# Sample tokens of an SSD scan in four row strips: one product for both parts of y, and state products as row tiles

## The chip, the cores and the metric

The kernel runs on one core of one Trainium2 chip. The metric is the device time of one execution in microseconds (us). A core has five engines that work side by side: PE (TensorE, the matrix products; its weight loads are listed apart as PEld), DVE (VectorE), ACT (ScalarE), POOL (GpSimd) and SP (SyncE, which here only issues DMAs). Before, three executions took 1623.5, 1624.79 and 1626.45 us, median 1624.79 us.

## The reference, cut to what matters

One inference step of a two-layer decoder: a Mamba-2 SSD layer, then a pooling layer, each with its own projections, gates and norms. It takes one prompt sequence of 1024 tokens and eight sample sequences of 8 new tokens each, so 64 sample tokens. The change touches the SSD scan of the sample tokens. For each of 32 heads (8 groups of 4, head dimension 64, state dimension 128), with `h` the state of one sequence:

```python
# h_t = exp(dt_t A) h_{t-1} + dt_t x_t B_t^T,   y_t = h_t C_t
y_intra = einsum('bctsgr,bcsgrp->bctgrp', CB[..., None] * decay, xdt)     # within the 8 tokens
chunk_states = einsum('bctgn,bctgr,bctgrp->bcgrpn', B, decay_end, xdt)    # what they add to the state
y_inter = einsum('bctgn,bctgr,bcgrpn->bctgrp', C, exp(acum), h_prev)      # what the old state gives
y = y_intra + y_inter;   h_final = chunk_decay * h_prev + chunk_states
```

The outputs include y of all tokens, and the new state of the prompt and of each of the eight sample sequences.

## The kernel before, in words

All activations lie with features on the 128 partitions and the 1088 tokens (1024 prompt, then 64 sample) along the row. The large projections run as three products of float32r halves (hi x hi, hi x lo, lo x hi; L182 to L184 and L980 to L982), one pass each; plain float32 products take two passes, and transposes one.

`ssd_layer` walks the eight groups g. For each, `scan_group` is a generator that is cut into steps by its yields, and between two steps the kernel puts one or more units of other work for PE: projections of later groups, and from group 4 on parts of the output projection (`FILL` says how many after each step; one projection unit is 24 products of 352 or 368 columns). So PE's queue alternates between short scan work and long runs of L182 to L184. The program text gives each instruction a place; the build's scheduler keeps dependent work in order and may put an instruction earlier in its engine's queue when its inputs are ready. Each engine then executes its queue strictly in order.

In a group, chunks 0 to 7 are 128 prompt tokens each, chunk 8 is the 64 sample tokens.

- `front(c)` (L534 to L576) makes for a chunk C·B (L545), the transposes of the two x tiles and of B (L549), the decay matrix M (L556 to L560) and the scaled x, `xd`, in two versions: times dt, and times dt and the decay to the chunk's end (L562). It takes a PSUM bank with the tag `tr` (two buffers).
- In chunk 8 the transposes are made twice, by `dup` (L434 to L437): the 64 tokens appear in partitions 0 to 63 and again in 64 to 127. The second copy is used for a product in two halves, hi and lo, in one pass over 128 rows.
- `states(c)` (L583) makes the prompt's chunk states S (L588) and the running state h: hd on POOL (L596), h on DVE (L597). `rows(c)` makes y of two chunks (L609, L613) with column tiles of 64.
- `sample_inter` (L617 to L633), after the rows of chunks 6 and 7: 8 products of 32-column tiles give Z, the old state times C, for four pairs of sequences in four strips of 32 partitions, of which 16 are used (L628); DVE scales it to `zsc` (L631).
- `back_sample` (L635 to L654) makes y of the sample tokens: in each of two PSUM banks (tag `y`, two buffers) two products of `xdt` and M over 64 rows (L641), then two of `zsc` and a selection matrix over 128 rows (L644); DVE adds the bank to x (L580). Then POOL multiplies the old states by their decay (L647, two instructions of 128x1024), ACT and DVE make `st`, hi in partitions 0 to 63 and lo in 64 to 127 (L652, L653).
- `state_sample(half)` (L656 to L667) runs twice, one step apart: for each of two pairs of sequences ACT makes two masked copies of `st` (L660), PE multiplies them by B in hi and lo (L663, 2 products of 128x512), DVE adds the bank (tags `S` and `y`) to the old state (L665); a DMA sends the half out (L666).
- After the first of them come the gate and its squares (L700 to L702), after the second the mean square (L708), the norm and its round trip through memory (L713, L716), and the next group has begun by then.

At the head of the kernel, `dt_phase` (L439 to L501) computes dt, its running sum and the decay, and transposes them for prompt chunks (L493) and, by `dup`, for the sample tokens (L496).

Of the kernel before, what the change touches and what calls it, by code (L numbers as in the profile page):

```python
# [7 lines left out]
F32 = mybir.dt.float32  # L8
F32R = mybir.dt.float32r
# [50 lines left out]
K_ID, K_MASK, K_SMASK, K_SEL9, K_SEL64, K_SCAN, K_SEQ, K_CNT = 0, 128, 256, 320, 330, 394, 714, 722  # L60
K_N = 782
# [36 lines left out]
class Build:  # L98
# [335 lines left out]
    def dup(self, out, ap):  # L434

        for h in (0, 64):
            self.nc.tensor.matmul(out[h:h + 64], ap, self.ident, start=True, stop=True, tile_position=(0, h))  # L437

    def dt_phase(self, ps):  # L439
# [48 lines left out]
        self.tk.update({("x", cc): self.gp.tile([P, 2, (128, 128, 32)[cc]], F32, tag=f"tkx{cc}", name=f"tkx{cc}") for cc in range(3)})  # L488
        for i, src in enumerate((ac, dt, de)):
# [6 lines left out]
            self.dup(ps[:, :128], src[:, 256:320])  # L496
            nc.vector.tensor_copy(ds[2], ps[:, 96:128])
# [6 lines left out]
    def scan_group(self, g, T):  # L504
# [29 lines left out]
        def front(c):  # L534
# [8 lines left out]
            nc.scalar.activation(ea[:, :, :L], acb, AF.Exp)  # L543
            pt = pp.tile([P, 512], F32, tag="tr", bufs=2, name=self.name("tr"))
            nc.tensor.matmul(pt[:L, 384:384 + L], B[:, tok], C[:, tok], start=True, stop=True)  # L545
            for i, t in enumerate((xs[0], xs[1], B)):
                o = pt[:, 128 * i:128 * i + 128]
                if c < 8:
                    nc.tensor.transpose(o, t[:, tok], self.ident)  # L549
                else:  # L550
                    self.dup(o, t[:, tok])

            M = gp.tile([P, 4, 128], F32, tag="M", bufs=3, name=self.name("M"))
            mask = self.kc[:L, K_MASK:K_MASK + 128] if c < 8 else self.kc[:64, K_SMASK:K_SMASK + 64]
            for r in range(4):
                nc.scalar.activation(M[:L, r, :L], acb[:L, r, :], AF.Relu, bias=tk["ac", cc][:L, col + r:col + r + 1], scale=-1.0)  # L556
            nc.scalar.activation(M[:L, :, :L], M[:L, :, :L], AF.Exp, scale=-1.0)
            cb = gp.tile([P, 128], F32, tag="cb", bufs=1, name=self.name("cb"))
            nc.vector.tensor_tensor(out=cb[:L, :L], in0=pt[:L, 384:384 + L], in1=mask, op=ALU.mult)
            nc.vector.tensor_tensor(out=M[:L, :, :L], in0=M[:L, :, :L], in1=cb[:L, :L].unsqueeze(1).to_broadcast([L, 4, L]), op=ALU.mult)  # L560
# [74 lines left out]
        def back_sample(F, zsc):  # L635
            tok, M, xdt, xde, Bt, _, ea = F
            for q in range(2):
# [1169 lines left out]
```

## Time and profile before

| | us |
|---|---|
| median of three executions (1623.5 to 1626.45) | 1624.79 |
| the profiled execution | 1625.1 |
| its span, first to last instruction | 1623.2 |
| PE busy | 1594.8 |
| DVE busy | 1290.4 |
| ACT busy | 815.2 |
| POOL busy | 497.8 |

The span is one execution on the chip as the hardware profiler saw it. A row of the timeline reads: start in us from the span's beginning, length in us, engine, line of the kernel, operation, output <- inputs by their names, shapes, how many instructions were merged into the row, and in brackets how long the engine was idle before it and what released it. For PEld, `128*64` means that the weights have 128 rows and 64 columns, and the merged row ends with the last load's end. A row of the groups (by line) ends in busy us and the mean ns of one instruction. A row of the windows view has the stretch, its length, and for PE, PEld, DVE, ACT and POOL the busy us with the number of instructions, then the granted clock of PE, the share of DMA time and GB/s.

### The profile page before, as it was taken

To read this page: it belongs to the slowest core of one execution; us is meant where nothing else is said; L and a number is where in the kernel's file an instruction comes from. 1 tells how busy PE (TensorE), PEld (TensorE's weight loads), DVE (VectorE), ACT (ScalarE), POOL (GpSimd) and SP (SyncE) were. 2 spreads that over 40 slices of the span, in tenths; PEclk is the share of its full clock that TensorE was granted. 3 is DMA by queue.
4 is the path that set the end of the run, shared out by engine and by line. 5 is a ranking of instruction groups with operands and counts; after the bars stand their busy time and mean duration, and the time that the engine had idled before them with its cause. 6 is when DMAs were issued, how large, how long until landed. Compare 5 with 4: busy or idle time off the path is not lost.

```text
span 1623.2 us, 30975 instructions
## 1 busy us (share of the span) xinstructions
PE 1594.8 (98%) x12061; PEld 1519.9 (94%) x12061; DVE 1290.4 (79%) x2140; ACT 815.2 (50%) x1565; POOL 497.8 (31%) x527
## 2 busy tenths in 40 slices
PE   8999999999999999999999999999999999999997
PEld 6899999998889898898899899999999999999997
DVE  6875779777787888889878867988899867577886
ACT  6653444357667667675555536632322233333364
POOL 0233556421221302120112222366667640000241
PEclk9999999999999999999999999999999999999999
DMA  9422232354554554678899633043333369665773
GB/s 348 163 99 82 94 110 71 107 198 128 194 161 159 166 190 134 215 226 295 272 333 313 216 130 112 29 143 111 103 108 100 134 206 362 181 159 182 160 175 121
DMA packets 122306, 275.60 MB, mean 170 GB/s; under 512 B 18192, under 2 KB 59312, under 8 KB 122160
## 3 DMA queue, kind: packets, MB, share of 16 engines
q1 hardware_dynamic: 118128, 260.91, 47.4%
q0 software_dynamic: 4032, 12.72, 4.5%
q8 instruction: 95, 1.56, 0.4%
q14 instruction: 51, 0.42, 0.1%
HBM read 201.12 MB, written 70.23 MB: 167 GB/s over the span
## 4 chain that ended last, share of the span: by engine, by line
PE 83%; DVE 6%; DMA 4%; issue 3%; ACT 3%; POOL 1%; SPq 0%; DVEq 0%; POOLq 0%; ACTq 0%
PE st L982 11%; PE st L980 11%; PE st L981 11%; PE mm L182 10%; PE mm L183 10%; PE mm L184 10%; PE op L1197 2%; PE op L1198 2%; PE op L1196 2%; PE y L609 2%; PE S L588 2%; PE y L613 1%; DMA acb<-acd 1%; PE am L253 1%; PE tr L549 1%
## 5 line engine op out<-in xcount | busy, mean ns | idle before, releaser
L982 PE MATMUL st<-hh,w 128*128 128x272 f32 x832 | 240.8, 289 | 2.3 <-DVE w L176 2.3
L980 PE MATMUL st<-hh,w 128*128 128x272 f32 x832 | 240.2, 289 | 0.0
L981 PE MATMUL st<-hl,w 128*128 128x272 f32 x832 | 239.8, 288 | 0.0
L982 PE MATMUL st<-t,w 128*128 128x272 f32 x624 | 179.5, 288 | 0.0
L980 PE MATMUL st<-t,w 128*128 128x272 f32 x624 | 179.5, 288 | 0.0
L981 PE MATMUL st<-t,w 128*128 128x272 f32 x624 | 179.2, 287 | 0.0
L182 PE MATMUL mm<-hh,wh 128*128 128x368 f32 (+1 forms) x528 | 178.2, 338 | 0.1
L183 PE MATMUL mm<-hl,wh 128*128 128x368 f32 (+1 forms) x528 | 173.4, 328 | 0.0
L184 PE MATMUL mm<-hh,wl 128*128 128x368 f32 (+1 forms) x528 | 173.4, 328 | 0.0
L174 ACT ACTIVATE w<-wr 128x512 fp32r<-128x512 f32 x104 | 65.7, 631 | 190.1 <-PE st L982 156.7
L982 PEld LDWEIGHTS st<-hh,w 128*128 128x128 f32 x832 | 156.4, 188 | 3.4 <-DVE w L176 3.4
L980 PEld LDWEIGHTS st<-hh,w 128*128 128x128 f32 x832 | 156.7, 188 | 0.3 <-issue 0.3
L981 PEld LDWEIGHTS st<-hl,w 128*128 128x128 f32 x832 | 156.8, 188 | 0.0
L596 POOL TENSOR_TENSOR hd<-h,cd 128x256 f32<-128x256 f32 x56 | 48.7, 870 | 347.8 <-DVE h L597 190.5
L182 PE MATMUL mm<-gh,wh 128*128 128x368 f32 (+1 forms) x384 | 129.1, 337 | 0.6 <-ACT raw L419 0.6
L1197 PE MATMUL op<-b,w 128*128 128x272 f32 x448 | 128.9, 288 | 0.7 <-DVE b L1126 0.7
L1196 PE MATMUL op<-b,w 128*128 128x272 f32 x448 | 129.4, 289 | 0.0
L1198 PE MATMUL op<-b,w 128*128 128x272 f32 x448 | 128.9, 288 | 0.0
L183 PE MATMUL mm<-gl,wh 128*128 128x368 f32 (+1 forms) x384 | 126.0, 328 | 1.1 <-DVE gl L743 1.0
L184 PE MATMUL mm<-gh,wl 128*128 128x368 f32 (+1 forms) x384 | 126.0, 328 | 0.0
L980 PEld LDWEIGHTS st<-t,w 128*128 128x128 f32 x624 | 117.7, 189 | 0.0
L982 PEld LDWEIGHTS st<-t,w 128*128 128x128 f32 x624 | 117.3, 188 | 0.0
(293 smaller groups left out, 4610.4 us busy)
## 6 DMA issues: line engine op xcount, KB each, us to landing
wr<-win SPq DMA_DIRECT2D x48, 512.0 KB, 3.9
acb<-acd SPq DMA_DIRECT2D x64, 256.0 KB, 4.0
wr<-pin SPq DMA_DIRECT2D x32, 512.0 KB, 3.8
wr<-pout SPq DMA_DIRECT2D x28, 512.0 KB, 3.9
x<-x1d SPq DMA_DIRECT2D x24, 544.0 KB, 6.6
x1d<-x SPq DMA_DIRECT2D x22, 544.0 KB, 5.5
wr<-pout POOLq DMA_DIRECT2D x20, 512.0 KB, 5.5
x<-xT SPq DMA_DIRECT2D x16, 544.0 KB, 6.1
```

What stands on the lines that cost most here:

```text
L174: self.nc.scalar.activation(hi, src, AF.Copy)
L182: nc.tensor.matmul(ps[:, :n], hi[:, k, :], ah[:, a:a + n], start=first, stop=False)
L183: nc.tensor.matmul(ps[:, :n], hi[:, k, :], al[:, a:a + n], start=False, stop=False)
L184: nc.tensor.matmul(ps[:, :n], lo[:, k, :], ah[:, a:a + n], start=False, stop=last)
L588: nc.tensor.matmul(S[:, 256 * i:256 * i + 256], Bt, xde.rearrange("p r q -> p (r q)"), start=True, stop=True)
L596: nc.gpsimd.tensor_tensor(out=hd, in0=h[-1], in1=cd.unsqueeze(2).to_broadcast([P, 4, 64]), op=ALU.mult)
L980: nc.tensor.matmul(ps[c][:, :QUART], hi[:, k], xh[:, t], start=(k == 0), stop=False)
L981: nc.tensor.matmul(ps[c][:, :QUART], hi[:, k], xl[:, t], start=False, stop=False)
L982: nc.tensor.matmul(ps[c][:, :QUART], lo[:, k], xh[:, t], start=False, stop=(k == 3))
L1196: nc.tensor.matmul(ps[:, :QUART], hi[:, k], xh, start=k == 0, stop=False)
L1197: nc.tensor.matmul(ps[:, :QUART], hi[:, k], xl, start=False, stop=False)
L1198: nc.tensor.matmul(ps[:, :QUART], lo[:, k], xh, start=False, stop=k == 7)
```

## The change

The 64 sample tokens are laid out as four pairs of sequences (16 tokens each) in four strips of 32 partitions. Each strip holds its 16 tokens twice. `twice` makes this layout on POOL, by a copy ahead of an ordinary transpose (`dup` goes).

- In `dt_phase`, three POOL copies (dt, its sum and the decay) and three ordinary transposes in place of three `dup`s. The dt version of x is set to zero in the first 16 rows of each strip (`K_LOW`).
- In chunk 8's `front`, three POOL copies (x, x, B), C·B over the doubled B (128 rows), three ordinary transposes. The mask `K_SMASK` is laid out for the strips; one more DVE instruction adds the selection matrix to the masked C·B, so that M holds the selection in the first 16 rows of each strip (there its exponential part is multiplied by it) and the intra-chunk matrix in the other 16.
- In `back_sample`, POOL adds `xdt` into `zsc` (called `xz`), and one product of 128 rows per head gives both parts of y: four products in place of eight.
- `st` is made by one instruction over all 128 partitions; the masked copies `xm` are two in place of eight, with the sign of hi and lo in the mask.
- `state_sample` runs once, where its first half was: eight products of 32 rows, 128 columns and 512 moving columns, at four row positions, each position with a PSUM bank of its own (tags `S`, `y`, `y`, `tr`); then four DVE additions and both DMAs. The step where the second half was keeps the mean square alone.

```diff
-    def dup(self, out, ap):
-
-        for h in (0, 64):
-            self.nc.tensor.matmul(out[h:h + 64], ap, self.ident, start=True, stop=True, tile_position=(0, h))
+    def twice(self, out, ap, eng):
+
+        eng.tensor_copy(out.rearrange("p (j h t) -> p j h t", j=4, h=2), ap.rearrange("p (j t) -> p j t", j=4).unsqueeze(2).to_broadcast([P, 4, 2, 16]))
...
+        t2 = self.raw_tile()[:, :384].rearrange("p (i m) -> p i m", i=3)
+        for i, src in enumerate((ac, dt, de)):
+            self.twice(t2[:, i, :], src[:, 256:320], nc.gpsimd)
...
-            self.dup(ps[:, :128], src[:, 256:320])
-            nc.vector.tensor_copy(ds[2], ps[:, 96:128])
+            nc.tensor.transpose(ps[:, :128], t2[:, i, :], self.ident)
+            if i == 1:
+                nc.vector.tensor_scalar(ds[2], ps[:, 96:128], self.kc[:, K_LOW:K_LOW + 1], None, op0=ALU.mult)
+            else:
+                nc.vector.tensor_copy(ds[2], ps[:, 96:128])
...
+            if c == 8:
+                xp = [gp.tile([P, 128], F32, tag=f"xp{i}", bufs=1, name=self.name("xp")) for i in range(3)]
+                for i, t in enumerate((xs[0], xs[1], B)):
+                    self.twice(xp[i], t[:, tok], nc.gpsimd)
             pt = pp.tile([P, 512], F32, tag="tr", bufs=2, name=self.name("tr"))
-            nc.tensor.matmul(pt[:L, 384:384 + L], B[:, tok], C[:, tok], start=True, stop=True)
+            nc.tensor.matmul(pt[:, 384:384 + L], B[:, tok] if c < 8 else xp[2], C[:, tok], start=True, stop=True)
...
-                if c < 8:
-                    nc.tensor.transpose(o, t[:, tok], self.ident)
-                else:
-                    self.dup(o, t[:, tok])
+                nc.tensor.transpose(o, t[:, tok] if c < 8 else xp[i], self.ident)
...
+            if c == 8:
+                nc.vector.tensor_tensor(out=cb[:, :L], in0=cb[:, :L], in1=self.kc[:, K_SEL64:K_SEL64 + 64], op=ALU.add)
...
-        def back_sample(F, zsc):
+        def back_sample(F, xz):
             tok, M, xdt, xde, Bt, _, ea = F
+            nc.gpsimd.tensor_tensor(out=xz, in0=xz, in1=xdt, op=ALU.add)
...
-                    nc.tensor.matmul(py[o, :64], xdt[:64, r, :], M[:64, r, :64], start=True, stop=False)
-                for rr in range(2):
-                    r, o = 2 * q + rr, slice(64 * rr, 64 * rr + 64)
-                    nc.tensor.matmul(py[o, :64], zsc[:, r, :], self.kc[:, K_SEL64:K_SEL64 + 64], start=False, stop=True)
+                    nc.tensor.matmul(py[o, :64], xz[:, r, :], M[:, r, :64], start=True, stop=True)
...
-            nc.vector.tensor_tensor(out=st[64:], in0=xv[64:], in1=st[64:].bitcast(F32), op=ALU.subtract)
-            return st, Bt
+            nc.vector.scalar_tensor_tensor(out=st, in0=xv, scalar=self.kc[:, K_LOW:K_LOW + 1], in1=st.bitcast(F32), op0=ALU.mult, op1=ALU.subtract)
+            xm = gp.tile([P, 2, 256], F32R, tag="xm", bufs=1, name=self.name("xs"))
+            for i in range(2):
+                nc.scalar.activation(xm[:, i], st.bitcast(F32), AF.Copy, scale=self.kc[:, K_SEQ + i:K_SEQ + i + 1])
+            return xm.rearrange("p b n -> p (b n)"), Bt
 
-        def state_sample(st, Bt, half):
-            for b2 in (2 * half, 2 * half + 1):
-                xm = gp.tile([P, 2, 256], F32R, tag="xm", bufs=2, name=self.name("xs"))
-                for i in range(2):
-                    nc.scalar.activation(xm[:, i], st.bitcast(F32), AF.Copy, scale=self.kc[:, K_SEQ + 2 * b2 + i:K_SEQ + 2 * b2 + i + 1])
-                S = pp.tile([P, 512], F32, tag=("S", "y")[b2 % 2], bufs=1 + b2 % 2, name=self.name("S"))
-                for i in range(2):
-                    nc.tensor.matmul(S, Bt[i], xm.rearrange("p b n -> p (b n)"), start=(i == 0), stop=(i == 1))
-                d = hsl[half][:, 512 * (b2 % 2):512 * (b2 % 2) + 512]
-                nc.vector.tensor_tensor(out=d, in0=d, in1=S, op=ALU.add)
-            nc.sync.dma_start(self.io["hsT"][g][:, 1024 * half:1024 * half + 1024], hsl[half][:, :1024])
-            self.slots.free(hsl[half])
+        def state_sample(xm, Bt):
+            S = [pp.tile([P, 512], F32, tag=t, bufs=b, name=self.name("S")) for t, b in (("S", 1), ("y", 2), ("y", 2), ("tr", 2))]
+            for i in range(2):
+                for j in range(4):
+                    o = slice(32 * j, 32 * j + 32)
+                    nc.tensor.matmul(S[j], Bt[i][o, :], xm[o, :], start=(i == 0), stop=(i == 1), tile_position=(32 * j, 0))
+            for j in (3, 2, 1, 0):
+                d = hsl[j // 2][:, 512 * (j % 2):512 * (j % 2) + 512]
+                nc.vector.tensor_tensor(out=d, in0=d, in1=S[j], op=ALU.add)
+            for i in range(2):
+                nc.sync.dma_start(self.io["hsT"][g][:, 1024 * i:1024 * i + 1024], hsl[i][:, :1024])
+                self.slots.free(hsl[i])
...
-        state_sample(*st, 0)
+        state_sample(*st)
...
-        state_sample(*st, 1)
```

More of the change, by code (lines that the diff above doesn't have):

```diff
@@ L1758, in _layout @@
     i = np.arange(64)
-    kc[:64, K_SMASK:K_SMASK + 64] = (i[None, :] >= i[:, None]) & (i[None, :] // 8 == i[:, None] // 8)
+    row = np.arange(P)
+    for j in range(4):
+        kc[32 * j + 16:32 * j + 32, K_SMASK:K_SMASK + 64] = ((i[None, :] >= i[:, None]) & (i[None, :] // 8 == i[:, None] // 8))[16 * j:16 * j + 16]
     for j in range(4):
@@ L1768, in _layout @@
     kc[:, K_SCAN:K_SCAN + 320] = sc
[L1769 removed]
+    kc[:, K_LOW] = row % 32 // 16
+    kc[:, K_SEQ:K_SEQ + 2] = (row[:, None] % 16 // 8 == np.arange(2)[None, :]) * (2.0 * (row[:, None] % 32 // 16) - 1)
     for gi, wd in enumerate(WINDOWS):
```

15 lines of the change are left out of this document (7 added, 8 removed).

## The prediction, made before the changed kernel was seen

> **What bounds the kernel now.** I read the page first, then PE's own waits, then the busy time of one stretch, then the weight loads one by one.
>
> ```profile
> span 1623.2 us, 30975 instructions
> ...
> PE 1594.8 (98%) x12061; PEld 1519.9 (94%) x12061; DVE 1290.4 (79%) x2140; ACT 815.2 (50%) x1565; POOL 497.8 (31%) x527
> ...
> PE 83%; DVE 6%; DMA 4%; issue 3%; ACT 3%; POOL 1%; SPq 0%; DVEq 0%; POOLq 0%; ACTq 0%
> ```
>
> PE is busy for 98% of the span and carries 83% of the chain that ended last; no other engine passes 79%. A busy PE can still hide waits, so I look at the scan alone, 355 to 936 us, by the windows view and by PE's waits (the longest row).
>
> ```profile
> 355.00:936.00 581.00, 574.51 (x4452) 520.20 (x4450) 480.26 (x794) 373.71 (x857) 109.82 (x166) 1.00 0.65 215
> ```
> ```profile
> PE S L588 <- ACT Bt L566: 1.9, 1, 1.9
> ```
>
> PE lacks work for 581.00 - 574.51 = 6.5 us in eight groups, and the longest single wait is 1.9 us. The granted clock is 1.00. So the scan is as long as PE's stream of instructions: one microsecond out of that stream is one microsecond off the end, as long as nothing new makes PE wait. I therefore price the change by the starts of weight loads (PEld), since a load starts when the array can take it, and the distance from one load to the next holds both the products and the drains between array shapes. All rows are from group 3 (or, for the first pair, group 3's chunks 4 and 6); the other groups have the same spacing.
>
> **The change part by part.**
>
> *Chunk 8's front.* The doubled transposes (L437, two column halves) become whole 128x128 transposes. The trace has both forms: the front of chunk 6 (no double, S to the rows' end) and that of chunk 8.
>
> ```profile
> 541.35 0.73 PEld L588 LDWEIGHTS S<-xd,Bt 128*128 128x128 f32 x4
> ...
> 542.43 0.36 PEld L549 LDWEIGHTS tr<-kc,xbc 128*128 128x128 f32 x3
> ...
> 544.86 0.19 PEld L182 LDWEIGHTS mm<-hh,wh 128*128 128x128 f32 x1 [0.17 <-issue]
> ```
> ```profile
> 554.67 0.73 PEld L588 LDWEIGHTS S<-xd,Bt 128*128 128x128 f32 x4 [0.41 <-issue]
> 555.73 0.13 PEld L545 LDWEIGHTS tr<-xbc,xbc 128*64 128x64 f32 x1 [0.33 <-PE S L588]
> ...
> 558.39 0.59 PEld L628 LDWEIGHTS Z<-h,ctm 128*32 128x32 f32 x16 [0.17 <-PE y L609]
> 559.39 0.19 PEld L182 LDWEIGHTS mm<-hh,wh 128*128 128x128 f32 x1 [0.41 <-issue]
> ```
>
> From the first S load to the end of the rows: 544.86 - 541.35 = 3.51 us with plain transposes, 558.39 - 554.67 = 3.72 us with the doubled ones. Saved: 0.21 us a group, 1.7 us in eight.
>
> *The sample's y.* Two products per half of y, in two array shapes, become one.
>
> ```profile
> 563.73 0.19 PEld L641 LDWEIGHTS y<-M,xd 64*64 64x64 f32 x4
> 564.00 0.20 PEld L644 LDWEIGHTS y<-kc,zsc 128*64 128x64 f32 x4
> 564.26 0.19 PEld L641 LDWEIGHTS y<-M,xd 64*64 64x64 f32 x4
> 564.52 0.20 PEld L644 LDWEIGHTS y<-kc,zsc 128*64 128x64 f32 x4
> 564.79 0.19 PEld L182 LDWEIGHTS mm<-hh,wh 128*128 128x128 f32 x1
> ```
>
> Today 564.79 - 563.73 = 1.06 us: four sets of four loads, each about 0.26 us. In a set the loads (0.13 us each) start within 0.06 us, so 0.20 us of each set is the drain to the next shape. After: two sets of L644's form (128*64) without a change of shape between them, 0.11 + 0.06 + 0.20 = 0.37 us. Saved: 0.69 us a group, 5.5 us.
>
> *The states.* Eight products of 128 rows by 512 columns, in two places, become eight of 32 rows in one place, four row tiles at a time. Before:
>
> ```profile
> 568.57 0.19 PEld L184 LDWEIGHTS mm<-hh,wl 128*128 128x128 f32 x1
> ...
> 569.37 0.19 PEld L663 LDWEIGHTS S<-xs,Bl 128*128 128x128 f32 x1
> 569.60 0.19 PEld L182 LDWEIGHTS mm<-hh,wh 128*128 128x128 f32 x1
> ```
> ```profile
> 583.34 0.19 PEld L184 LDWEIGHTS mm<-hh,wl 128*128 128x128 f32 x1
> ...
> 584.14 0.19 PEld L663 LDWEIGHTS S<-xs,Bl 128*128 128x128 f32 x1
> 584.70 0.16 PEld L708 LDWEIGHTS ms<-z,ones 128*32 128x32 f32 x8 [0.37 <-issue]
> 585.29 0.30 PEld L545 LDWEIGHTS tr<-xbc,xbc 128*128 128x128 f32 x2 [0.44 <-issue]
> ```
> ```profile
> 553.24 0.19 PEld L184 LDWEIGHTS mm<-hh,wl 128*128 128x128 f32 x1
> 553.66 0.16 PEld L253 LDWEIGHTS am<-wr,scp 128*32 128x32 f32 x8 [0.23 <-issue]
> ```
>
> The first half puts 569.60 - 568.57 = 1.03 us where the stream has 0.17 (one load to the next): 0.86 us. The second puts 584.70 - 583.34 = 1.36 us where, without it, the stream would go to narrow products as at 553.24, in 0.42 us: 0.94 us. Together 1.80 us a group. After, entering another shape costs 0.42 - 0.17 = 0.25 us. The block itself no row shows: no row tile runs in this kernel. The nearest rows are column tiles: Z's 16 loads are four rounds of four tiles, and last 559.39 - 558.39 = 1.00 us with their drain; a pass like L588's, one after another, takes about 0.215 us, so four tiles do run at once and the drain is 1.00 - 4 x 0.215 = 0.14 us. A narrow load takes 0.11 us, a full-width one 0.19 us.
>
> ```profile
> L628 PEld LDWEIGHTS Z<-h,ctm x128: 106/109/110, 408.1 to 919.8; 128*32 128x32 f32 x128
> ```
>
> If row tiles do the same, two rounds of 512 columns (569.37 to 569.60: 0.23 us a product) and the drain are 0.61 us, and 0.69 us with the longer load (0.19 against 0.11 us). Then the states cost 0.25 + 0.69 = 0.94 us and save 0.86 us a group, 6.9 us. I take this value. From the other side there are two bounds. If the eight full-width loads go one after another, 0.11 us apart as the three of L549 do, the block is 7 x 0.11 + 0.56 (last L663 load to the next shape) = 1.33 us: saved 0.22 us a group, 1.8 us. If the products do not overlap either, it is 7 x 0.23 + 0.56 = 2.17 us: lost 0.62 us a group, 5.0 us.
>
> The Trainium skill, "TensorE: Matmul & The Clock Gate", section "Measured speedup vs the span model", gives four row tiles of 512 columns 3.07 times, not four. By that the eight products (8 x 0.23 = 1.84 us) would take 0.60 us instead of 0.46, and the sum would end 1.1 us later, an estimate from that page; no run here shows a row tile yet.
>
> *The head of the kernel.* dt_phase has three doubled transposes of its own.
>
> ```profile
> 129.55 0.19 PEld L982 LDWEIGHTS st<-hh,w 128*128 128x128 f32 x1
> 129.90 0.20 PEld L437 LDWEIGHTS tr<-kc,raw 128*64 128x64 f32 x4 [0.15 <-DVE tka L494]
> ...
> 130.27 0.25 PEld L980 LDWEIGHTS st<-hh,w 128*128 128x128 f32 x1
> ...
> 130.95 0.14 PEld L493 LDWEIGHTS tr<-kc,raw 128*128 128x128 f32 x1
> 131.07 0.19 PEld L982 LDWEIGHTS st<-hh,w 128*128 128x128 f32 x1
> ```
>
> One costs 130.27 - 129.55 = 0.72 us less the usual 0.13; a plain transpose 0.12. Saved: 3 x 0.47 = 1.4 us.
>
> *What is added elsewhere* is priced by these rows.
>
> ```profile
> L596 POOL TENSOR_TENSOR hd<-h,cd 128x256 f32<-128x256 f32 x56 | 48.7, 870 | 347.8 <-DVE h L597 190.5 <-DVE h L593 107.6 <-ACT M L556 29.3
> ...
> L823 POOL COPY u<-spl 128x120 f32<-128x120 f32 x16 | 7.8, 487 | 1.2 <-DMA spl<-spool 1.2
> ```
> ```profile
> 557.05 0.42 DVE L597 TENSOR_TENSOR h<-hd,S 128x256 f32<-128x256 f32 x1 [0.73 <-POOL hd L596]
> ...
> 559.60 4.52 POOL L647 TENSOR_TENSOR h<-h,ea 128x1024 f32<-128x1024 f32 x2 [0.26 <-DMA wr<-win]
> ...
> 560.00 0.42 DVE L631 TENSOR_TENSOR zsc<-Z,eap 128x256 f32<-128x256 f32 x1
> ```
> ```profile
> L665 DVE TENSOR_TENSOR h<-h,S x32: 669/680/689, 421.0 to 936.0; 128x512 f32<-128x512 f32 x32
> ```
>
> POOL gets three copies a group (about 0.49 us each, as L823's of nearly this size) and the sum xz (0.87 us, L596's size). The copies read x and B, which lie ready long before chunk 8, and they wait only for the last group's transposes; cost nothing. If all three stood ahead of the hd that lets L597 free the S bank, they would delay Z by 1.47 us less its cover, 558.39 - 557.47 - 0.21 = 0.71: 0.8 us a group, 6 us. The sum xz is a new wait in front of y: zsc ends at 560.42; POOL is then in the first of the two multiplications of L647 (2.26 us each), which ends at 561.86; xz ends near 562.8, and y is due at 563.73 - 0.21 = 563.52. Cost nothing, with 0.7 us of cover. Behind xz stands only the second L647, due ten microseconds later. ACT loses six of eight L660 copies a group, off the path. DVE gets one small addition and does the four adds of L665 (0.68 us each) in a row, 2.7 us instead of twice 1.4; the banks they hold are next asked for by the mean square at 584.70, and chunk fronts have a second tr buffer. Cost nothing; if a unit's product waited for DVE it would be at most 1.4 us a group. The two hsT DMAs leave together, a unit earlier for the second, and on SP they wait for the last of the four adds (up to 1.4 us longer than now); behind them stand the next weight and acb loads.
>
> ```profile
> acb<-acd SPq DMA_DIRECT2D x64, 256.0 KB, 4.0
> ```
>
> An acb load lands 4.0 us after its issue and is issued a whole chunk (at least one unit, from 559.39 to about 563.7) ahead; 1.4 us later it is still in time or nearly so: cost nothing, at most 1 us a group.
>
> **Sum:** 1.7 + 5.5 + 6.9 + 1.4 = 15.5 us. The profiled execution took 1625.1 us (span 1623.2 and 1.9 around it), 0.3 us above the median of the three runs, 1624.79. 1625.1 - 15.5 = 1609.6 us.
>
> **The rivals.**
> 1. *Loads one after another* in the row tiles: 1.7 + 5.5 + 1.8 + 1.4 = 10.4 saved, 1614.7 us. For it: full-width loads never start under 0.11 us apart in this trace. Against it: the tiles' loads go to different rows, and column tiles load 0.01 us apart (eight of L253's within 0.16). The Trainium skill, same page, section "LDWEIGHTS (loading the stationary operand)", says that a load's time goes by its columns and not its rows; 0.11 us for 32 columns and 0.19 for 128 agree, and whether such loads overlap by row tiles no run here shows yet.
> 2. *Row tiles do not run at once*, so that part does not do what it says: 3.6 saved, 1621.5 us. Against it: Z's tiles do overlap.
> 3. *xz behind both multiplications* of L647: they end at 564.12, xz at 564.99, y about 1.5 us late; 12 us in eight groups, 1621.6 us. Against it: zsc is ready 1.4 us before the second one starts, and xz stands ahead of it in program order.
> 4. *Slower:* the same place, with the three copies for the next group also ahead of xz (POOL runs such copies early: ctm's are made right after Z). Then y is 1.5 + 1.47 = 3.0 us late, 24 us in eight groups: 1625.1 - 15.5 + 24 = 1633.6 us. It decides from a delay of 15.5 / 8 = 1.9 us a group.
>
> **How the numbers follow.** Forecast 0.62; rival 1 0.14; rival 2 0.05; rival 3 0.07; rival 4 0.07; 0.05 for a reordering of PE's stream that I can't name, split over all sides. A change of 0.2%, 3.2 us, is about what a measurement of this kernel can tell from none. Forecast and rival 1 are faster by more, rivals 2 and 3 lie at the edge (same), rival 4 is slower: faster 0.79, same 0.13, slower 0.08. The range begins at 1605, the forecast with 4 of the scan's 6.5 us of waits gone too, and ends at 1620, past rival 1 and with the 5 us that the copies or the adds could cost; it leaves out rivals 2 to 4.
>
> **What would show it.** Chunk 8's front should have one shape up to the rows, L609 0.2 us earlier; y's block should be near 0.37 us; the states' loads should start nearly together in two fours, with 0.7 us to the next load, not 1.3 or 2.2; POOL's xz should end before y's first load; PE's waits in the scan should stay near 6.5 us. A wait of y's load for POOL, or of a transpose for the copies, makes the prediction wrong.

## The result, and the profile after

The changed kernel takes 1617.54 us (median of five runs, 1615.95 to 1620.23), the kernel before, timed beside it, 1624.79 (1623.39 to 1626.45): ratio 0.9958, interval [0.9947, 0.9969], 7.3 us less. The forecast was 15.5 us less. The profiled execution took 1620.23 us. In its page the busy share of TensorE is as before:

```profile
span 1618.5 us, 30648 instructions
...
PE 1581.7 (98%) x11916; PEld 1506.4 (93%) x11916; DVE 1288.2 (80%) x2148; ACT 796.5 (49%) x1517; POOL 500.8 (31%) x562
```

The code numbers the groups from 0, and so does this part; what the prediction calls group 3 is the third one, group 2. Line numbers are the changed kernel's (S is L596, h L605, Z L636, xz L645, the sample's y L650, the state products L670, their additions L673, the stores L675, gh and gl L749 and L750).

**Where the time went.** The windows view, cut at the first weight load of each group's mean square, so that a stretch is a number of whole groups: first before, then after. The first row of each is groups 1 to 3, the second groups 4 to 7.

```profile
434.41:659.96 225.55, 225.51 (x1760) 202.58 (x1759) 185.94 (x283) 154.03 (x348) 46.41 (x81) 1.00 0.52 168
...
659.96:935.55 275.59, 270.43 (x2086) 246.59 (x2085) 235.81 (x420) 163.07 (x372) 47.55 (x56) 1.00 0.79 266
```
```profile
432.23:652.21 219.98, 219.89 (x1708) 196.98 (x1707) 186.39 (x286) 146.79 (x330) 45.22 (x93) 1.00 0.53 172
...
652.21:929.23 277.02, 265.16 (x2019) 242.59 (x2018) 234.80 (x422) 154.80 (x350) 55.29 (x73) 0.99 0.78 266
```

Groups 1 to 3 are 225.55 - 219.98 = 5.57 us shorter, 1.86 us each, where the forecast had 0.21 + 0.69 + 0.86 = 1.76. Groups 4 to 7, which should have given 7 us, are 1.4 us *longer*. TensorE has 5.3 us less to do there, but lacks work for 277.02 - 265.16 = 11.9 us instead of 5.2, and its granted clock is 0.99. The profiled execution is the slowest of its five: its span is 4.7 us shorter, so 10.8 of the forecast's 15.5 us are missing in it. These four groups miss 8.5 of them. Up to the first cut 2.2 us are saved where dt_phase and group 0 should have saved 3.2, and the stretch behind the last cut, which the change does not touch, is 1.6 us longer (687.7 before, 689.3 after). Two more profiles of the changed kernel (c0 and c1 below) have 221.2 us for groups 1 to 3, 1.5 us less a group, and 276.1 and 278.0 us for groups 4 to 7.

The same pieces as the prediction's, in group 2:

```profile
550.67 0.73 PEld L596 LDWEIGHTS S<-xd,Bt 128*128 128x128 f32 x4 [0.41 <-issue]
...
554.13 0.59 PEld L636 LDWEIGHTS Z<-h,ctm 128*32 128x32 f32 x16 [0.17 <-issue]
...
559.48 0.31 PEld L650 LDWEIGHTS y<-M,zsc 128*64 128x64 f32 x8
559.86 0.19 PEld L182 LDWEIGHTS mm<-hh,wh 128*128 128x128 f32 x1
...
564.08 0.19 PEld L670 LDWEIGHTS S<-xs,Bt 32*128 32x128 f32 x4 [0.24 <-issue]
564.18 0.19 PEld L670 LDWEIGHTS S<-xs,Bl 32*128 32x128 f32 x4
564.75 0.19 PEld L182 LDWEIGHTS mm<-hh,wh 128*128 128x128 f32 x1 [0.37 <-issue]
```

S to the rows' end 554.13 - 550.67 = 3.46 us (forecast 3.51), y 0.38 (0.37), the states 0.67 (0.69), with 0.24 to enter their shape (0.25). Four loads of 0.18 us each end 0.19 us after the first began, so they do run together. Each price was right, and the blocks keep it in all eight groups: from first load to the next shape's load y's takes 0.38 us and the states' 0.67 us in each. What failed is that all of it would come off the end.

**What TensorE waits for in groups 4 to 7**, before and after (rows: us in all, times, longest):

```profile
PEld S L588 <- ACT Bt L566: 2.7, 3, 2.1
...
PEld mm L183 <- DVE gl L743: 1.3, 1, 1.3
```
```profile
PEld mm L183 <- DVE gl L750: 4.1, 2, 2.9
PEld y L650 <- POOL zsc L645: 4.0, 3, 2.2
...
PEld S L596 <- ACT Bt L574: 2.0, 2, 1.8
```

The wait for gl has grown threefold, and that of y for xz is new. In group 2 xz stands between the two multiplications, as the prediction had it. In groups 5 to 7 the build's scheduler put it behind both; this is group 6:

```profile
555.34 2.02 POOL L653 TENSOR_TENSOR h<-h,ea 128x1024 f32<-128x1024 f32 x1 [0.26 <-issue]
557.32 1.18 POOL L645 TENSOR_TENSOR zsc<-zsc,xd 128x256 f32<-128x256 f32 x1
558.47 1.93 POOL L653 TENSOR_TENSOR h<-h,ea 128x1024 f32<-128x1024 f32 x1
```
```profile
853.96 4.17 POOL L653 TENSOR_TENSOR h<-h,ea 128x1024 f32<-128x1024 f32 x2 [0.26 <-PE Z L636]
858.09 1.76 POOL L645 TENSOR_TENSOR zsc<-zsc,xd 128x256 f32<-128x256 f32 x1
```

xz ends at 859.85, and y's first load, due at about 857.7, starts at 859.91. The wait costs more than its own length, as the loads behind it and the windows view of two stretches show:

```profile
861.20 0.20 PEld L182 LDWEIGHTS mm<-gh,wh 128*128 128x128 f32 x1
861.36 0.33 PEld L183 LDWEIGHTS mm<-gl,wh 128*128 128x128 f32 x1
861.66 0.33 PEld L184 LDWEIGHTS mm<-gh,wl 128*128 128x128 f32 x1
```
```profile
731.60:735.00 3.40, 2.84 (x11) 2.84 (x12) 3.40 (x4) 0.00 (x0) 0.00 (x0) 0.50 0.59 201
861.30:864.70 3.40, 3.40 (x14) 3.40 (x13) 2.01 (x4) 1.11 (x1) 0.00 (x0) 0.50 0.80 265
```

For 3.4 us the granted clock is 0.50 and products follow each other at 0.30 us instead of 0.16: some 1.5 us lost behind this wait, an estimate (3.4 us hold 11 products at 0.30, each 0.14 us longer), and somewhat less behind the one at 732, where TensorE is busy for 2.84 of the 3.40 us. The kernel before has no such window in its scan.

**What stands behind the gl wait at 732**, on ACT, DVE, SP, DVE and PEld of the changed kernel:

```profile
707.71 0.63 ACT L548 ACTIVATE ea<-acb 128x512 f32<-128x512 f32 x1 [1.75 <-DMA acb<-acd]
```
```profile
720.50 1.23 DVE L360 SCALAR_TENSOR_TENSOR xbc<-raw,raw 128x1024 f32<-128x1024 f32 x1 [0.98 <-ACT raw L359]
...
721.78 1.28 DVE L673 TENSOR_TENSOR h<-h,S 128x512 f32<-128x512 f32 x2
```
```profile
SPq L533 <- ACT cd L582: 3.9, 1, 3.9
```
```profile
718.85 0.37 SPq L533 DMA_DIRECT2D acb<-acd  x1
719.34 0.90 SPq L1528 DMA_DIRECT2D x<-xT  x2
720.66 2.77 SPq L675 DMA_DIRECT2D hsT<-h  x2
```
```profile
730.82 1.29 DVE L750 TENSOR_TENSOR gl<-gr,gh 128x1088 fp32r<-128x1088 f32 x1 [3.01 <-issue]
```
```profile
732.16 0.29 PEld L183 LDWEIGHTS mm<-gl,wh 128*128 128x128 f32 x1 [2.94 <-DVE gl L750]
```

ACT waits 1.75 us for an acb load, so the convolution's raw (L359), which stands behind it in that queue, is late for DVE; the second pair of state additions stands behind L360 on DVE; the second store leaves at 723.1; and gl, whose buffer is that of the stored states, begins 7.7 us later. The profile names no releaser for gl here; the experiments do. But late additions alone don't make gl wait, since gl stands behind them on DVE: without its wait of 3.01 us it would begin at 727.81, 6.0 us behind L673. What it waits for is the store's own 7.7 us. SP shows what stands ahead of the stores: the next acb load, which waits 3.9 us until ACT has read the buffer that it overwrites (one of two), and two x loads of 544 KB behind it, the first one 1.3 us ahead of the first store. That these loads make the store slow is read from the order; no run moves them alone. The prediction had looked at the acb load in group 2 and written "cost nothing, at most 1 us a group"; the wait of gl for a store it doesn't name, though the kernel before has 1.3 us of it (the row above).

### The profile page after: what moved, and what is told of

Read it like the earlier page. It is cut to its first block, busy times and chain, and to the rows that moved or that the text cites. A ratio compares the mean times of both kernels' runs of the same rounds, so it can differ in the third digit from the quotient of the medians.

```text
span 1618.5 us, 30648 instructions
## 1 busy us (share of the span) xinstructions
PE 1581.7 (98%) x11916; PEld 1506.4 (93%) x11916; DVE 1288.2 (80%) x2148; ACT 796.5 (49%) x1517; POOL 500.8 (31%) x562
```

## The experiments

Every kernel ran beside the kernel before on its chip. The columns: median, that of before, ratio with its 95% interval, and of the profiled execution the length of groups 4 to 7, what TensorE lacked there (length less busy), and half-clock windows in the scan. The three profiles of the changed kernel differ by 1.9 us in the length of groups 4 to 7, so a smaller difference in that column says little.

| run | us | before | ratio | groups 4-7 | lack | windows |
|---|---|---|---|---|---|---|
| before | 1624.79 | | 1 | 275.6 | 5.2 | 0 |
| changed | 1617.54 | 1624.79 | 0.9958 [0.9947, 0.9969] | 277.0 | 11.9 | 2 |
| c0, changed again | 1619.98 | 1626.66 | 0.9950 [0.9931, 0.9970] | 276.1 | 12.7 | 1 |
| c1, changed again | 1620.80 | 1626.92 | 0.9958 [0.9944, 0.9971] | 278.0 | 12.8 | 2 |
| e1 | 1619.11 | 1628.08 | 0.9940 [0.9922, 0.9958] | 275.8 | 11.8 | 1 |
| e2 | 1620.06 | 1628.08 | 0.9948 [0.9931, 0.9964] | 278.0 | 12.0 | 2 |
| e3 | 1621.36 | 1628.08 | 0.9955 [0.9939, 0.9971] | 277.4 | 11.4 | 2 |
| e4 | 1624.35 | 1628.08 | 0.9975 [0.9963, 0.9987] | 278.8 | 11.1 | 1 |
| e5 | 1623.16 | 1626.66 | 0.9976 [0.9961, 0.9991] | 279.7 | 7.5 | 1 |
| e6 | 1626.66 | 1626.66 | 0.9995 [0.9982, 1.0008] | 277.1 | 13.6 | 1 |
| e7 | 1625.98 | 1626.66 | 0.9983 [0.9968, 0.9998] | 274.5 | 11.2 | 1 |
| e8 | 1616.70 | 1626.93 | 0.9938 [0.9924, 0.9952] | 276.0 | 10.9 | 2 |
| e9 | 1617.09 | 1626.93 | 0.9938 [0.9922, 0.9953] | 276.5 | 10.5 | 2 |
| e10 | 1613.55 | 1626.93 | 0.9922 [0.9906, 0.9939] | 273.6 | 9.1 | 1 |
| e11 | 1628.21 | 1626.93 | 1.0010 [0.9997, 1.0023] | 278.5 | 7.8 | 0 |
| e12 | 1612.14 | 1626.92 | 0.9918 [0.9900, 0.9935] | 269.6 | 8.3 | 0 |
| e13 | 1613.19 | 1626.92 | 0.9919 [0.9903, 0.9935] | 274.0 | 9.8 | 1 |
| e14 | 1625.65 | 1626.40 | 0.9991 [0.9978, 1.0005] | 275.0 | 4.8 | 0 |
| e15 | 1618.37 | 1626.40 | 0.9943 [0.9925, 0.9962] | 273.9 | 10.3 | 1 |
| e16 | 1611.48 | 1626.40 | 0.9898 [0.9880, 0.9916] | 271.8 | 8.2 | 1 |

My first theory was that the waits in sight (xz, gl) with their half-clock windows eat the gain; its rival, that groups 4 to 7 are as long as their transfers make them, so that a wait taken away comes back elsewhere.

**e1, xz ahead of both multiplications**, in all groups; only POOL's order differs.

```diff
-            nc.gpsimd.tensor_tensor(out=xz, in0=xz, in1=xdt, op=ALU.add)
+            ins = nc.gpsimd.tensor_tensor(out=xz, in0=xz, in1=xdt, op=ALU.add)
...
+                with self.tc.issue_after(ins.ins):   # around the L653 instructions
```

> Only POOL's order changes: the sum xz now stands ahead of both multiplications of the old states, in every group; the queues of PE, DVE, ACT and SP are those of the changed kernel. Theory (the wait for xz costs time in groups 5, 6 and 7, where xz stood behind both multiplications): the waits of y's load for POOL there (0.26 + 1.86 + 0.81 = 2.9 us) go, and with the longest of them the half-clock window that followed it at 861.3 us (3.4 us, in which 11 products took 0.30 instead of 0.17 us, 1.5 us): about 4 us faster than the changed kernel, 1613 to 1614 us by its median of 1617.5. Rival (groups 4 to 7 are held by their transfers, share of DMA time 0.67 to 0.87, and whatever PE saves is waited for elsewhere): same as the changed kernel, 1617.5 us, with the waits moved to other lines.

The three y waits are gone, but others stand in their place: in groups 4 to 7 of this run's waits,

```profile
PEld mm L183 <- DVE gl L750: 4.2, 2, 3.1
PEld S L596 <- ACT Bt L574: 4.1, 3, 2.4
PEld Z L636 <- issue: 2.3, 2, 2.1
```

and the lack is 11.8 us as in the changed kernel; groups 1 to 3 now lack 2.9 us too, where the changed kernel's three profiles lack 0.1 to 1.2. By itself the xz wait explains at most 2 or 3 us.

**e2, xz on DVE**: L645 with `nc.vector` in place of `nc.gpsimd`.

> The sum xz moves from POOL to DVE, right behind zsc (0.42 us there); PE's order is that of the changed kernel. Theory: as with xz put first, y's waits in groups 5 to 7 and one half-clock window go, about 4 us faster than the changed kernel, 1613 to 1614 us; POOL's multiplications then run without a break. Rival: 1617.5 us.

No gain over the changed kernel that could be told. The edit did not take y's waits away: TensorE now waits for DVE's xz 0.5 to 0.8 us in seven of eight groups, 4.2 us in all, where it waited 2.9 us for POOL's; and the gl wait is 3.3 us.

**e3, the second half of the states stored and freed first**: `for i in (1, 0)` in the loop of L674 to L676.

> The second half of the new states is stored and its buffer freed ahead of the first (its additions come first anyway); all else as in the changed kernel, with PE's order changed in some 13 rows near 725 us alone. After group 4 a part of the output projection (gl) takes a buffer that the store of the new states must leave first. Theory: that buffer is now the one whose store left first (issued at 720.66, landed at 728.31, against 723.08 and about 730.8), so the 2.65 us wait of PE at 732.2 mostly goes, and with it the half-clock window at 731.6 (4 to 10 products at 0.30 us): 2.5 to 4 us faster than the changed kernel, 1613.5 to 1615 us. Rival (the wait is for the transfer of gr itself or for another engine, not for that buffer): 1617.5 us and PE still waits over 2 us at gl.

My expectation fell: the scheduler then put the product that needs gl earlier as well, and TensorE waits 3.0 us at 728.3. But DVE's row now names what gl waits for:

```profile
726.97 1.29 DVE L750 TENSOR_TENSOR gl<-gr,gh 128x1088 fp32r<-128x1088 f32 x1 [2.82 <-DMA hsT<-h]
```

**e4, no row tiles**: the same eight products with all 128 rows.

```diff
-                    nc.tensor.matmul(S[j], Bt[i][o, :], xm[o, :], start=(i == 0), stop=(i == 1), tile_position=(32 * j, 0))
+                    nc.tensor.matmul(S[j], Bt[i], xm, start=(i == 0), stop=(i == 1))
```

> The eight state products take all 128 rows each instead of 32, one after another in one array shape (this leaves out the separation of the four strips, so each bank holds the sum over all of them). PE's order is that of the changed kernel. Theory (row tiles run four at once and save what the prediction says): a block of eight costs 8 x 0.23 = 1.9 us in place of 0.25 + 0.67 = 0.92 us, so groups 0 to 3 become 0.95 us longer each and the whole kernel 5 to 8 us slower than the changed one, 1622.5 to 1625.5 us. Rival (the saving comes from y and the transposes alone): within 2 us of the changed kernel.

Groups 1 to 3 take 223.00 us, 1.0 us a group more than with row tiles (0.6 against c0 and c1), and the block of eight 1.80 us instead of 0.67: running four at once is worth that, less the change of shape. Groups 4 to 7 take only 1.7 us more than the changed kernel's for the four, not 4, and the whole kernel 3 to 4 us more by the ratios, where 5 to 8 were expected: it seems that these groups hide work as they hid savings, but 1.7 us is within the spread of that column.

**e5 and e6, the change in groups 0 to 3 alone, or 4 to 7 alone.**

```diff
+NEW = (0, 1, 2, 3)     # e6: (4, 5, 6, 7)
...
-        st = back_sample(F, zsc)
+        new = g in NEW
+        st = (back_sample if new else back_old)(F, zsc)
```

> The change in groups 0 to 3 alone; groups 4 to 7 sample as the kernel before does, and both layouts' transposes are kept in the preparation of dt, which costs some 1.5 us more there than the change does. Theory A (the gain of the late groups is waited away, because these groups end when their transfers and their buffers let them): groups 0 to 3 give their 1.87 us each, 7.5 in sum, less the 1.3 to 1.5 that the preparation of dt no longer saves, so the ratio to the kernel before is 0.9955 to 0.997 and the time lies 0 to 2 us above the changed kernel's. Rival B (each late group gains as well, and one accident - a wait at one place, the clock's half-speed windows - eats it): the late groups without the change have the 7.0 us of waits that the kernel before has there and not the changed kernel's 13.9, and lack 7.5 of gain, so nothing differs in the sum either, but the load stalls of TensorE in groups 4 to 7 are then at 7 us and the windows at half clock are gone. The split between the two is made with the run of the late groups alone.

> The change in groups 4 to 7 alone; groups 0 to 3 sample as the kernel before does, and both layouts' transposes are kept. Theory A: the four late groups keep their lengths (275 to 278 us from the mean square of group 3 to that of group 7), so the time is within 2 us of the kernel before or up to 1.5 us above it (the extra preparation of dt). Rival B (the late groups gain 1.87 each unless the early ones have been shortened, because the transfers of the late groups are due at fixed times after the start): here the early groups are as late as before, the transfers are as far ahead as before, and the late groups gain some 6 to 7 us: 1618 to 1620.

Alone, the late groups' half gives nothing (0.9995) and the early half 3.5 us (both keep the doubled transposes of dt_phase, so its 1.4 us are in neither). In e6 the late groups start as late as in the kernel before and their gain is lost all the same, so it isn't only an earlier start that loses it. In e5 the late groups, whose code is that of before, got 4 us longer; a window at half clock at 903 us and waits for ACT's Bt are there, but why this run has them I can't say.

**e7, e8, e11: the buffers of the states given back after the mean square**, so that gl takes others: in all groups with e1's edit (e7), in group 4 alone (e8), and in group 4 of the kernel before (e11).

```diff
-                self.slots.free(hsl[i])
+                self.slots.free(*(() if g in (4,) else (hsl[i],)))
...
-        rst = self.slots.get("rs")
+        rst = (self.slots.get("rs"), self.slots.free(*(hsl if g in (4,) else ())))[0]
```

> The sample's decayed product ahead of both multiplications of h0, and the two state buffers given back only after the step of the mean square, so that the next group's high and low parts of g never wait for the store of the states. Theory A (the late groups are held by several things at once): the wait of 3 us at the start of group 5 goes, others take its place, and the time is within 2 us of the changed kernel. Rival B (this wait and the window of half clock behind it are the loss): 3 to 4.5 us less than the changed kernel, some 1613 to 1614.5.

> In group 4 alone the two state buffers are given back after the mean square's step and not right after their store, so that the high and low parts of g that open group 5 (L749, L750) take other buffers and wait for no store; the orders of TensorE and GpSimd are the changed kernel's but for a few products. Theory B (a handful of places eat the late groups' gain, and this is the largest): the wait of 2.96 us at 732 goes, the 0.66 us behind it and the half-clock window of 3.4 us that opens there (1.45 to 1.7 us lost) go with it: 3 to 4.5 us less than the changed kernel, some 0.993 of the kernel before. Theory A (the late groups are as long as their transfers make them): within 1.5 us of the changed kernel, 0.995 to 0.996, and the stalls stand elsewhere in groups 5 to 7.

> The kernel before, with its buffers of group 4 given back late in the same way; the orders of its TensorE, VectorE and GpSimd are the same. Its own wait for the store at the start of group 5 is 1.28 us and opens no half-clock window. Theory B: 1 to 1.5 us less than the kernel before (0.999 to 1.0), so the place costs the changed kernel 2 to 3 us more than the kernel before. Theory A: no difference.

In e7 the edit reordered the engines in all groups and TensorE waits for ACT's Bt in the early ones (0.8 to 2.8 us a group), so it settles little; its groups 5 to 7 are 197.2 us, 4.0 less than the changed kernel's. e8 is the clean form. Its gl wait is gone, so gl had waited for the store; but the next load is late as well, first on DVE and then on PEld:

```profile
731.84 0.60 DVE L771 SCALAR_TENSOR_TENSOR x<-mm,gat,x 128x368 f32<-128x368 f32 x1 [1.13 <-DMA x<-xT]
```
```profile
732.49 0.19 PEld L182 LDWEIGHTS mm<-gh,wh 128*128 128x128 f32 x1 [2.53 <-DVE x L771]
```

The gain is 0.9938 against 0.9950 to 0.9958 for the changed kernel, intervals that overlap. e11: no gain in the kernel before; gl's wait is gone there too, and TensorE waits 2.6 us for ACT's raw instead.

**e9 and e10: xz first in groups 5 to 7 alone** (e1's edit with `if g in (5, 6, 7)`), and both this and e8's.

> The sum xz ahead of both multiplications of h0 on GpSimd in groups 5 to 7 alone (groups 0 to 4 stay as in the changed kernel; no other engine's order differs). Theory B: the y waits of 0.29, 1.89 and 0.85 us go, and the half-clock window at 861 with them: 3 to 4.5 us less than the changed kernel. Theory A: the waits come back as others in the same groups (as in the run with all eight groups), within 1.5 us of the changed kernel.

> Both edits: the buffers of group 4 given back late, and xz first in groups 5 to 7. Theory B: the sum of the two, 6 to 8 us less than the changed kernel, 1609.5 to 1611.5 or 0.990 to 0.992 of the kernel before, and the four late groups' length from mean square to mean square falls from 277 to 269 to 271 us. Theory A: within 2 us of the changed kernel, and the length stays above 275 us.

One place gives 0.9938, both 0.9922, which is 13.4 us under the kernel before, against 6 to 7 for the changed kernel: well over half of what was missing, and between the two values that were expected. What waits are left begin with DMA. The longest of ACT, in e10 and, in the same place, in the kernel before:

```profile
896.59 0.21 ACT L582 ACTIVATE cd<-acb 128x4 f32<-128x4 f32 x1 [3.35 <-DMA acb<-acd]
```
```profile
907.78 0.21 ACT L574 ACTIVATE cd<-acb 128x4 f32<-128x4 f32 x1 [2.95 <-DMA acb<-acd]
```

TensorE waits 2.2 us behind the first and 1.9 behind the second. So the prediction's line on acb came under test.

**e12, acb loads two chunks ahead**: a third buffer (room for it made by sharing and dropping others) and one changed line.

```diff
-                t = gp.tile([P, 4, 128], F32, tag="acb", bufs=2, name=self.name("acb"))
+                t = gp.tile([P, 4, 128], F32, tag="acb", bufs=3, name=self.name("acb"))
...
-            load_ac(c + 1) if c < 8 else None
+            load_ac(c + 2) if c < 7 else None
...
-        load_ac(0)
+        load_ac(0), load_ac(1)
```

> The changed kernel with a third acb buffer and each acb load issued two chunks ahead in place of one (the doubled x and B share the buffer of the masked copies for the room); no computation differs. In the trace of the kernel with both edits ACT waits 3.35 us for an acb load at 896.59 and TensorE 1.99 us behind it, and the kernel before shows the same pair (2.95 and 2.15 us). Theory A' (what is left of the late groups' loss is late acb loads): the waits of S for ACT's Bt in group 6 and 7 go, 1.4 us here and the half-clock window where there is one; 1 to 3 us less than the changed kernel. Rival: DMA time is the limit there (share 0.86 to 0.94), so that another transfer becomes late by as much: within 1 us.

0.9918, on the chip on which the changed kernel has 0.9958: by the ratios 6.5 of the 8.7 us that were missing there, from an edit that touches no product, and more than the 1 to 3 us that were expected. Groups 4 to 7 fall from 277.0 to 269.6 us, below the 275.6 of before. The chain that led to gl shows why; ACT, SP, then DVE:

```profile
703.49 0.62 ACT L548 ACTIVATE ea<-acb 128x512 f32<-128x512 f32 x1
```
```profile
713.41 0.81 SPq L1528 DMA_DIRECT2D x<-xT  x2
716.65 2.93 SPq L675 DMA_DIRECT2D hsT<-h  x2
```
```profile
717.94 1.28 DVE L673 TENSOR_TENSOR h<-h,S 128x512 f32<-128x512 f32 x2
...
723.89 1.28 DVE L750 TENSOR_TENSOR gl<-gr,gh 128x1088 fp32r<-128x1088 f32 x1
```

L548 has no gap ahead of it (it had waited 1.75 us), and L673 follows it after 14.45 us as it did after 14.07. The second store leaves at 719.2, where the changed kernel's left at 723.1. gl stands 5.95 us behind L673, as it would have in the changed kernel, but it no longer waits: the store has landed by 723.89, within 4.7 us of its issue and not 7.7. The x loads now leave 3.2 us ahead of the first store and not 1.3, since the acb load ahead of them no longer waits for cd. So the rival, DMA time as such, fell: there was time for the loads, if acb's is issued a chunk earlier.

**e13, e14, e15, e16**: e10's edits with the loads ahead; the kernel before with the loads ahead; the room for the third buffer without moving a load; and the loads ahead with xz first in groups 5 to 7.

> Late free in group 4, xz first in groups 5 to 7, and acb loads two chunks ahead. Theory A': the waits at 875.7 (0.73), 878.6 (1.18) and 897.0 us (1.99) and the half-clock window at 897 (1.5 us) of the kernel with both edits go: 3 to 5 us less than that kernel, 0.989 to 0.9905 of the kernel before. Rival: within 1 us of the kernel with both edits, 0.9915 to 0.993.

> The kernel before with the same third acb buffer and loads two chunks ahead (room made by putting st into a constant table that is no longer used, one buffer of Bl and one of scv in place of two); TensorE's order is the kernel before's. Theory P (late acb loads held the late groups of both kernels alike): it gains as the changed kernel did, 5 to 7 us (0.9955 to 0.997), and the change is worth 8 us with the loads ahead as without. Theory Q (the kernel before had enough work between two chunks to cover the loads, and only the change ran into them): 0 to 2 us (0.999 to 1.0), and the change is worth 13 to 15 us once the loads are ahead, as forecast.

> The changed kernel with only the room made for the third acb buffer (the doubled x and B share the buffer of the masked copies, one buffer of Bl) and no load moved. If the acb loads are what gained the 7 us, this stands within 1.5 us of the changed kernel, 0.995 to 0.9965. If the shared buffer is (its copies can no longer run ahead of hd on GpSimd), it gains the 7 us by itself, 0.991 to 0.993.

> acb loads two chunks ahead, and xz first in groups 5 to 7, without the late free. If the waits add, the y waits of 0.31, 1.95 and 0.89 us go: 2 to 3 us less than with the loads alone, 0.9895 to 0.9905. If they replace one another, as they did with all three edits: within 1 us of the loads alone, 0.9915 to 0.9925.

Groups 4 to 7 by the windows view: e12, e14, e16 (its profiled execution, 1614.16 us, is its longest of six).

```profile
650.63:920.27 269.64, 261.33 (x2019) 239.64 (x2018) 236.16 (x422) 154.04 (x350) 58.15 (x73) 1.00 0.79 273
```
```profile
660.37:935.33 274.96, 270.14 (x2086) 246.59 (x2085) 235.16 (x420) 162.20 (x372) 49.31 (x56) 1.00 0.78 266
```
```profile
651.25:923.04 271.79, 263.61 (x2018) 240.80 (x2017) 235.44 (x422) 153.53 (x350) 60.24 (x73) 0.99 0.79 270
```

- e14 tells the two theories of the loads apart. The kernel before, with TensorE's order unchanged, gains 0.1% [-0.05, 0.22]: it lacked only 5.2 us in these groups, and still lacks 4.8. Late loads were not what held it, though ACT waits for them about as long in its groups 4 to 7 as in the changed kernel's (13.0 and 14.7 us). They hold the changed kernel.
- e16: 0.9898, which is 16.6 us [13.7, 19.5] under the kernel before (15 us by the medians), and the y waits are gone. It beats both kernels, and its interval holds the forecast's 15.5 us. It overlaps e12's interval too, and the lack is e12's, 8.2 us, with other waits in the place of y's: what xz adds to the loads is not shown. Measured against e14, which has the loads ahead too, 0.9898 / 0.9991 = 0.9907: the change is worth 15 us when the loads are early and xz is in its place. Where they come off is not all in sight: in the profiled execution groups 4 to 7 are 3.2 us shorter than e14's, where the forecast has 7.
- e13 shows that cures don't add: with all three edits the time is e12's. In e12 gl had already ceased to wait, and freeing its buffer late moves other things.
- e15, room only, is 0.9943, between the two values that were expected: its interval holds the changed kernel's ratio, and reaches 0.9925. So some 0.4 of e12's gain (0.0015 of 0.0040) could be the room's, by the interval's end most of it. Its trace shows what the room does not do: ACT waits 15.3 us for acb in groups 4 to 7 (14.7 in the changed kernel, 7.3 in e12), and the long gl wait stands as there, with its half-clock window; in e12 both are gone:

```profile
730.98 0.29 PEld L183 LDWEIGHTS mm<-gl,wh 128*128 128x128 f32 x1 [2.94 <-DVE gl L750]
```

## Why the prediction was right or wrong

- **Chunk 8's front, y, the states: right**, to 0.05 us each in group 2, and to 0.1 us in the period of groups 1 to 3 (to 0.3 in c0's and c1's). Rivals 1 and 2 fell: loads and products of four row tiles run at once. The Trainium skill, "TensorE: Matmul & The Clock Gate", section "Measured speedup vs the span model", has 3.07 times for four row tiles of 512 columns; by that the block would take 0.60 + 0.14 + 0.08 = 0.82 us, an estimate from that page; the trace has 0.67, which is below it. The forecast's 0.69 is in part luck: it takes 0.215 us for a pass of L588, which none of its rows shows; by chunk 6's loads, (542.11 - 541.35) / 4 = 0.19 us, the drain is 0.24 and the block 0.78 us.
- **dt_phase: right.** Its transposes now cost 131.39 - 131.13 - 0.13 = 0.13 us each, where they were 0.59:

```profile
131.13 0.19 PEld L989 LDWEIGHTS st<-hh,w 128*128 128x128 f32 x1
131.30 0.14 PEld L498 LDWEIGHTS tr<-kc,raw 128*128 128x128 f32 x1
131.39 0.19 PEld L987 LDWEIGHTS st<-hh,w 128*128 128x128 f32 x1
```

- **The step that failed** is "one microsecond out of that stream is one microsecond off the end, as long as nothing new makes PE wait", with the new waits put at nothing from what group 2 shows: xz "cost nothing, with 0.7 us of cover", and "An acb load ... is still in time or nearly so: cost nothing, at most 1 us a group". In group 2 both hold. In groups 4 to 7 DMA's share is 0.78 to 0.79 instead of 0.52, and output-projection work with buffers of its own is mixed in. There 7.0 us were forecast and -1.4 measured: 6.7 us more waits and two half-clock windows. The longest of the waits is gl's for the store of the states, and for it the prediction has no term. Getting acb two chunks ahead, with the room for it, brought 6.5 us back, and with xz in its place too the time is near the forecast's. That e16's 16.6 us lie so near 15.5 is in part luck: its groups 4 to 7 still lack 8.2 us, where the forecast left the 5.2 of before.
- **Rival 3** (xz behind both multiplications) came true in three groups of eight. Its argument against, "xz stands ahead of it in program order", was wrong: program order doesn't bind the scheduler. It cost 2.9 us of waits (0.3, 1.9 and 0.8), not 12, and a half-clock window; xz itself took 0.72 to 1.76 us, where 0.87 was forecast.
- "PE's waits in the scan should stay near 6.5 us": 355 to 936 us now has 581.00 - 568.60 = 12.4 us.

```profile
355.00:936.00 581.00, 568.60 (x4356) 515.29 (x4355) 483.27 (x808) 358.01 (x812) 118.34 (x199) 0.99 0.65 218
```

- **Rival 4 did not come**: the copies take 0.29 us each in the median, 1.15 at most (0.49 forecast), and no wait of TensorE names them.

Open: why no other small edit (e1 to e3, e8, e9) gave the sum of the waits that it removed, beyond that the next load, an x or an acb, was late by nearly as much; the share of e15; and why the store takes 7.7 us.

## What to carry to other kernels

The price of a block can hold in every stage, as here, and still not come off the end in every stage: before multiplying by the number of groups, compare the DMA share and the lack of work of each. A saving on the busy engine is kept only as far as the loads are issued ahead of the *new* schedule; when a large part of it vanishes, follow the longest new wait back through the in-order queues, the one that issues DMAs too, and not only to the instruction named last. A buffer that a store must leave is a wait with a price of its own. Where the order is the scheduler's, pin what an argument rests on.

## What the runs showed of the hardware

- **A wait of TensorE can cost some 1.5 us beyond its length** (the estimate above). In the scan of all 20 traces (430 to 960 us) there are 22 windows at half clock (3.41 us, one of 6.8), each behind a wait of TensorE. Of 66 waits of 0.7 to 1.4 us none opened one; of 14 of 1.4 to 1.7 us one, of 23 of 1.7 to 2.0 us seven, of 11 of 2.0 to 2.5 us five, of 10 longer ones nine. The same wait may or may not open one: 859.9 us in the changed kernel (1.86 us idle) did, 853.1 in e12 (1.87) did not. The Trainium skill, "TensorE: Matmul & The Clock Gate", section "HAM oscillation — how this bites in real kernels", gives as the rule that gaps of over some 3.4 us of an idle TensorE must be avoided; by this trace gaps from 1.6 us on can cost a window.
- **POOL's times vary by over two with the same form**, hd and xz below (min, median, max in ns); one hd of 1.46 us, at 850.74, lay beside DVE's wl split (L140, 850.51 to 851.73); whether that made it long no run shows.

```profile
L604 POOL TENSOR_TENSOR hd<-h,cd x56: 608/613/1681, 370.4 to 911.8; 128x256 f32<-128x256 f32 x56
```
```profile
L645 POOL TENSOR_TENSOR zsc<-zsc,xd x8: 719/1189/1764, 410.8 to 919.2; 128x256 f32<-128x256 f32 x8
```

- **A store took 7.7 us** from issue to landing (the one at 720.7, issued 0.9 and 1.3 us behind two x loads), where the median of those whose landing the profile shows is 3.1 us.
